# Seven more layer-1 blocks beside the gate matrix, kept in DRAM until the expert loop uses them

## The chip, the cores and the metric

The kernel runs on one core of one Trainium2 chip. The metric is the device time of one execution in microseconds. Of the kernel before there are three timed runs, and one execution was profiled; all durations below are of that one.

## The reference, cut to what matters

One encoder block over 512 tokens of width 1024: two kinds of attention, then PEER, a product-key retrieval of single-neuron experts. The change touches only PEER. Each token has 8 heads, each of which picks 16 of 128 x 128 = 16384 experts:

```python
def chunk(args):
    xc, ic, gc = args
    uc = u[ic]
    act = jnp.einsum("cd,ced->ce", xc, uc)
    hid = jax.nn.gelu(act, approximate=False) * gc
    return jnp.einsum("ce,ced->cd", hid, v[ic])
```

## The kernel before, in words

The matmuls of float32 operands are made of three products of a rounded high part (hi) and a low remainder (lo). `load_split` loads one 128x1024 tile into `raw` by SP's queue, rounds it on ScalarE (L82, `whi`) and subtracts on VectorE or GpSimd (L84, `wlo`).

PEER is computed in two ways at once. For the first 320 tokens (T1) every expert is computed densely, in 128 blocks of 128 experts. **Layer 1** of block j (`layer1`, L610) is 24 matmuls of 128x320 (L100 to L102) of `u_blk[j]` with the tokens, and a Gelu on ScalarE into a tile `ge` (L617). **Layer 2** of block j (`layer2`, L894) multiplies `ge` by the gate matrix's block (`hd`, L888), splits it into `hh` and `hl`, and adds it times `v_blk[j]` into six accumulators (18 matmuls of 128x512, L901), for 384 tokens. For the other tokens the chosen experts' rows are fetched: 64 gathers from `u_rows` (`ug` with `codeX`, VectorE's L629) for 64 tokens, whose second layer is in the dense one, and 128 gathers of u and 128 of v rows (`vg`, VectorE's L637) for the last 128 tokens.

The stages that matter here follow each other:

- **The gate stage.** The gate matrix of 384 tokens is built in 24 chunks (`ch`) of 4 groups of 4 tokens: VectorE makes one-hot tiles (`oh`, L834), GpSimd and ScalarE in turn scale them by the gate (L842, L840), TensorE multiplies them (`ps_s`, L846), ScalarE copies to `stg` (L847), and each chunk is written to DRAM (`gdram`, 1 MB). The 51 remaining `codeX` gathers are spread over the first 72 groups. Beside it layer-1 blocks are computed ahead (`backlog`); their `ge` tiles stay in SBUF, in a pool `blp` of NB = 47 buffers. 21 blocks are made before the gate stage; NG = 17 are spread over its first 80 groups, their low parts on VectorE and GpSimd in turn; NP = 5 stand between group 80 and group 81, all on GpSimd; and the last 4 behind the last group.
- Group 81 needs a transpose of `hx` (L825), the result of the `codeX` gathers. It is placed on TensorE behind the NP blocks.
- **The expert loop** (L960). For j below 47 an iteration is layer 2 alone, with `ge` from SBUF. From 47 on it also has layer 1 of the next block. Every iteration loads `v_blk` (512 KB, two buffers `raw2`, low part on VectorE) and, with 2 of 8, part of the gate tile `gtl` back from DRAM. `gather_to` (L964) paces the 256 gathers by `gw`: 1.174 in an iteration of layer 2 alone, 2.25 times that in one with layer 1. `ug` and `vg` have three buffers each.

The order on each engine is made by a scheduler at build time, which sorts by a simulated time and keeps what the waits, `issue_after` and `keep_in_program_order` demand. Each engine then runs its list strictly in order, and SP's queue does too.

## Time and profile before

| | |
|---|---|
| timed runs | 1695.65, 1700.76, 1707.4 us; median 1700.76 |
| profiled execution | 1701.23 us |
| its span, first to last instruction | 1699.2 us |
| TensorE busy in the span | 1601.0 us (94%) |
| VectorE, ScalarE, GpSimd busy | 1310.4, 807.6, 779.5 us |
| bytes moved | 407.44 MB, mean 240 GB/s |

Busy time of one engine is the union of its instructions. The matmuls of the gate stage appear as two rows each, so its 384 are 768 in the trace. A row of a window says for each engine how long it was busy in that stretch, so that busy against length shows which engine the stage runs on.

### The profile page before, as it was taken

The numbers are of one execution on the slowest core, as the hardware profiler recorded it, in microseconds if no ns is written. First come the engines' busy times: TensorE is split into PE (matmuls) and PEld (weight loads), VectorE is DVE, ScalarE is ACT, GpSimd is POOL, SyncE is SP. The second block draws the span as 40 slices with busy tenths as digits, with TensorE's granted clock in tenths as the row PEclk, the third lists the DMA queues.
The fourth block names the chain that finished last, engine by engine and source line by source line (L and its number), as shares of the span: only waits on it lengthen the run. The fifth ranks groups of instructions, "written<-read, shape, count | busy, mean of one in ns | idle before, by whom it ended". The sixth has DMA issues, their size and how long they took to land.

```text
span 1699.2 us, 25986 instructions
## 1 busy us (share of the span) xinstructions
PE 1601.0 (94%) x9390; PEld 1435.4 (84%) x9390; DVE 1310.4 (77%) x2594; ACT 807.6 (48%) x1523; POOL 779.5 (46%) x653
## 2 busy tenths in 40 slices
PE   8989999998999858889899999999999999999997
PEld 7878988788999758789778778988888888888986
DVE  7376766546799989997568887888888888888875
ACT  5446565434333248788633333444444444434334
POOL 2543221123789977776213333444444445443341
PEclk9999999999999979999999999999999999999999
DMA  7523211333222549997589999999999999999982
GB/s 249 148 57 92 83 67 50 100 99 131 86 93 92 196 167 345 346 362 272 198 284 326 327 337 319 322 345 331 353 337 344 334 355 334 343 339 316 315 295 102
DMA packets 162482, 407.44 MB, mean 240 GB/s; under 512 B 21297, under 2 KB 72881, under 8 KB 159282
## 3 DMA queue, kind: packets, MB, share of 16 engines
q1 hardware_dynamic: 114848, 235.63, 40.2%
q0 software_dynamic: 47360, 169.89, 28.7%
q8 instruction: 74, 1.21, 0.3%
q14 instruction: 54, 0.44, 0.1%
q10 hardware_dynamic: 146, 0.27, 0.0%
HBM read 374.02 MB, written 30.87 MB: 238 GB/s over the span
## 4 chain that ended last, share of the span: by engine, by line
PE 72%; DVE 12%; DMA 5%; ACT 4%; issue 4%; POOL 3%; SPq 0%; ACTq 0%; POOLq 0%; DVEq 0%
PE acc L901 29%; PE ps_mm L100 12%; PE ps_mm L102 11%; PE ps_mm L101 11%; DMA vg<-in_v_blk_dram,codeV 3%; PE ps_s L846 2%; DVE oh L834 1%; ACT stg L847 1%; DMA ug<-in_u_rows_dram,codeX 1%; PE ps_o L100 1%; PE ps_o L102 1%; PE ps_o L101 1%; ACT whi L82 1%; PE ps_t L365 1%; POOL oh L842 1%
## 5 line engine op out<-in xcount | busy, mean ns | idle before, releaser
L82 ACT ACTIVATE whi<-raw 128x1024 fp32r<-128x1024 f32 x322 | 341.4, 1061 | 475.5 <-PE ps_mm L101 197.5
L84 DVE TENSOR_TENSOR wlo<-raw,whi 128x1024 fp32r<-128x1024 f32 x234 | 287.2, 1229 | 146.1 <-ACT whi L82 144.6
L100 PE MATMUL ps_mm<-xah,whi 128*128 128x320 f32 x1152 | 361.6, 314 | 11.0 <-ACT ge L617 9.4
L102 PE MATMUL ps_mm<-xah,wlo 128*128 128x320 f32 x1152 | 359.4, 312 | 6.8 <-POOL wlo L84 4.0
L101 PE MATMUL ps_mm<-xal,whi 128*128 128x320 f32 x1152 | 358.3, 311 | 0.0
L84 POOL TENSOR_TENSOR wlo<-raw,whi 128x1024 fp32r<-128x1024 f32 x88 | 214.7, 2441 | 283.3 <-ACT whi L82 235.5
L626 POOL DMA_INDIRECT ug<-in_u_rows_dram,codeU x128 | 159.7, 1248 | 261.1 <-DVE ug L629 241.1
L634 POOL DMA_INDIRECT vg<-in_v_blk_dram,codeV x128 | 174.6, 1364 | 221.7 <-DVE yg L637 197.3
L901 PE MATMUL acc<-whi,hh 128*128 128x512 f32 x756 | 243.0, 397 | 3.0 <-ACT hh L90 3.0
L901 PE MATMUL acc<-wlo,hh 128*128 128x512 f32 x756 | 239.4, 396 | 0.0
L901 PE MATMUL acc<-whi,hl 128*128 128x512 f32 x756 | 234.4, 395 | 0.0
L100 PEld LDWEIGHTS ps_mm<-xah,whi 128*128 128x128 f32 x1152 | 218.6, 190 | 16.2 <-ACT ge L617 10.7
L102 PEld LDWEIGHTS ps_mm<-xah,wlo 128*128 128x128 f32 x1152 | 218.2, 189 | 9.5 <-POOL wlo L84 5.0
L101 PEld LDWEIGHTS ps_mm<-xal,whi 128*128 128x128 f32 x1152 | 218.6, 190 | 3.6
L637 DVE SCALAR_TENSOR_TENSOR yg<-vg,hidg,yg 128x1024 f32<-128x1024 f32 x128 | 164.2, 1283 | 9.6 <-DMA vg<-in_v_blk_dram,codeV 9.6
L901 PEld LDWEIGHTS acc<-wlo,hh 128*128 128x128 f32 x756 | 142.3, 188 | 34.8
L901 PEld LDWEIGHTS acc<-whi,hl 128*128 128x128 f32 x756 | 141.6, 188 | 34.7 <-DVE hl L92 0.4
L901 PEld LDWEIGHTS acc<-whi,hh 128*128 128x128 f32 x756 | 138.8, 188 | 31.2 <-ACT hh L90 3.5
L629 DVE SCALAR_TENSOR_TENSOR ug<-ug,xg 128x1024 f32<-128x1024 f32 x128 | 155.8, 1219 | 2.6 <-DMA ug<-in_u_rows_dram,codeU 2.6
L846 PE MATMUL ps_s<-oh 128*128 128x128 f32 x768 | 107.2, 290 | 32.8 <-POOL oh L842 16.3
L846 PEld LDWEIGHTS ps_s<-oh 128*128 128x128 f32 x768 | 98.8, 196 | 39.9 <-POOL oh L842 21.6
L90 ACT ACTIVATE hh<-hd 128x384 fp32r<-128x384 f32 x128 | 66.4, 520 | 114.1 <-DVE hd L888 113.0
(277 smaller groups left out, 2891.2 us busy)
## 6 DMA issues: line engine op xcount, KB each, us to landing
raw<-in_u_blk_dram SPq DMA_DIRECT2D x128, 512.0 KB
raw<-in_v_blk_dram SPq DMA_DIRECT2D x128, 512.0 KB
gdram<-stg SPq DMA_DIRECT2D x24, 1024.0 KB
gtl<-gdram SPq DMA_DIRECT2D x64, 384.0 KB
raw<-in_w_in_dram SPq DMA_DIRECT2D x34, 512.0 KB
raw<-in_w_q_dram SPq DMA_DIRECT2D x16, 512.0 KB
x_t<-in_x_dram SPq DMA_DIRECT2D x8, 512.0 KB
raw<-in_w_o_dram SPq DMA_DIRECT2D x8, 512.0 KB
```

Of the source, the lines that this page charges most:

```text
L82: act(hi, raw, AF.Copy)
L84: eng.tensor_tensor(out=lo, in0=raw, in1=hi.bitcast(F32), op=ALU.subtract)
L90: last_hi[0] = act(hi, src, AF.Copy, scale=scale)
L100: mm(ps, ah, bh, start=i == 0, stop=False)
L101: mm(ps, ah, bl, start=False, stop=False)
L102: last = mm(ps, al, bh, start=False, stop=i == n - 1)
L626: i_ = pool.indirect_dma_start(out=t, out_offset=None, in_=u_src, in_offset=bass.IndirectOffsetOnAxis(ap=code[:, p:p + 1], axis=0))
L629: return vec.scalar_tensor_tensor(out=t, in0=t, scalar=1.0, in1=mul, op0=ALU.mult, op1=ALU.mult, accum_out=dst[:, p:p + 1])
L634: i_ = pool.indirect_dma_start(out=t, out_offset=None, in_=v_src, in_offset=bass.IndirectOffsetOnAxis(ap=codeV[:, p:p + 1], axis=0))
L637: vec.scalar_tensor_tensor(out=yg, in0=t, scalar=hidg[:, p:p + 1], in1=yg, op0=ALU.mult, op1=ALU.add)
L846: gm = mm(ps[:, z * P:(z + 1) * P], oh[:, 0, z], oh[:, 1, z], start=True, stop=True)
L901: mm(accs[tt][hf], st_[:, ts_], mv[:, hf * S:(hf + 1) * S], start=j == 0 and st_ is hh and mv is vh, stop=False)
```

## The change

Seven more blocks, 47 to 53, are computed before the loop. SBUF keeps only the first 47; the seven go through a two-buffer tile `sge` to a DRAM tensor `sdram`, by ScalarE's own DMA queue, and `load_ge` brings each back by SP's queue two iterations ahead, into `dq`'s `ge` tile of two buffers. So the loop has 54 iterations of layer 2 alone in place of 47, and seven fewer with layer 1. Of the seven, five are spread over the first 80 groups (NG 17 to 22), one stands with the NP blocks (5 to 6), one behind the last group (4 to 5). In the spread part every third block has its low part on VectorE, where it was every second: 8 of 17 before, 8 of 22 now. `gw` rises to 256 / (54 + 2.25 x 69) = 1.223.

```diff
+NS = 7
+    sdram = dp.tile([NS, P, T1], F32, name="sdram")
-        ge = keep.tile([P, T1], F32, name="ge")
+        ge = keep.tile([P, T1], F32, name="ge") if j < NB or j >= NB + NS else stp.tile([P, T1], F32, name="sge", bufs=2)
         with tc.issue_after(last_hi[0].ins) if j < 2 else ExitStack():
             act(ge, ps[:, :T1], AF.Gelu)
+        if NB <= j < NB + NS:
+            nc.scalar.dma_start(sdram[j - NB], ge)
         return ge
...
-                if nbl[0] < NB:
+                if nbl[0] < NB + NS:
...
-        NP = 5
-        NG = NB - 4 - NP - nbl[0]
+        NP = 6
+        NG = NB + NS - 5 - NP - nbl[0]
...
-                        backlog(1, (vec, pool)[nbl[0] % 2])
+                        backlog(1, (vec, pool, pool)[nbl[0] % 3])
...
-            backlog(NB, vec)
+            backlog(NB + NS, vec)
...
-        return gelu_bl[j] if j < NB else layer1(j, dq, vec)
+        return gelu_bl[j] if j < NB else ge.pop(j) if j < NB + NS else layer1(j, dq, vec)
+
+    def load_ge(j):
+        if NB <= j < NB + NS:
+            ge[j] = dq.tile([P, T1], F32, name="ge")
+            nc.sync.dma_start(ge[j], sdram[j - NB])
...
-    gw = (2 * P) / (NB + 2.25 * (NK - NB - 5))
+    gw = (2 * P) / (NB + NS + 2.25 * (NK - NB - NS - 5))
     for j in range(NK - 1):
         cur, vcur = nxt, vnx
         vnx = vget(j + 1)
+        load_ge(j + 2)
         nxt = hidden(j + 1, get_ge(j + 1))
...
-            gather_to(int(gw * (min(j + 1, NB) + 2.25 * max(0, j + 1 - NB))))
+            gather_to(int(gw * (min(j + 1, NB + NS) + 2.25 * max(0, j + 1 - NB - NS))))
```

In the changed file the lines below `NS = 7` stand 1 to 10 lower. On GpSimd, early in the gate stage, the list before is (L842 scales a one-hot tile, L626 is a gather, L84 a layer-1 block's low part):

```order
L842 TENSOR_TENSOR oh<-oh,pk 128x512
L626 DMA ug<-in_u_rows_dram,codeX 128x1024
L84 TENSOR_TENSOR wlo<-raw,whi 128x1024
L626 DMA ug<-in_u_rows_dram,codeX 128x1024
L842 TENSOR_TENSOR oh<-oh,pk 128x512
L626 DMA ug<-in_u_rows_dram,codeX 128x1024
L842 TENSOR_TENSOR oh<-oh,pk 128x512
L626 DMA ug<-in_u_rows_dram,codeX 128x1024
L842 TENSOR_TENSOR oh<-oh,pk 128x512
L626 DMA ug<-in_u_rows_dram,codeX 128x1024 x2
L842 TENSOR_TENSOR oh<-oh,pk 128x512
```

and at the same place, with the change (L846 scales, L630 gathers, L85 is the low part):

```order
L846 TENSOR_TENSOR oh<-oh,pk 128x512
L630 DMA ug<-in_u_rows_dram,codeX 128x1024
L85 TENSOR_TENSOR wlo<-raw,whi 128x1024
L630 DMA ug<-in_u_rows_dram,codeX 128x1024 x2
L846 TENSOR_TENSOR oh<-oh,pk 128x512
L85 TENSOR_TENSOR wlo<-raw,whi 128x1024
L846 TENSOR_TENSOR oh<-oh,pk 128x512
L630 DMA ug<-in_u_rows_dram,codeX 128x1024
L846 TENSOR_TENSOR oh<-oh,pk 128x512
L630 DMA ug<-in_u_rows_dram,codeX 128x1024 x2
L846 TENSOR_TENSOR oh<-oh,pk 128x512
```

A second low part now stands among the scalings and gathers of the same stretch. On ScalarE, from the last copies of the gate stage to the first split of the loop, the list before is (`raw_9269` is the first `raw2` tile):

```order
L847 ACTIVATE stg<-ps_s 128x4x128 x2
L617 ACTIVATE ge<-ps_mm 128x320 x2
L82 ACTIVATE whi<-raw_9269 128x1024
L617 ACTIVATE ge<-ps_mm 128x320 x2
L889 ACTIVATE hd<-gtl 128x64 x2
L90 ACTIVATE hh<-hd 128x384 x2
```

and with the change, from the first write on:

```order
L621 DMA sdram<-sge 128x320
L619 ACTIVATE sge<-ps_mm 128x320
L621 DMA sdram<-sge 128x320
L619 ACTIVATE sge<-ps_mm 128x320
L621 DMA sdram<-sge 128x320
L619 ACTIVATE sge<-ps_mm 128x320
L621 DMA sdram<-sge 128x320
L619 ACTIVATE sge<-ps_mm 128x320
L621 DMA sdram<-sge 128x320
L83 ACTIVATE whi<-raw_9508 128x1024
L893 ACTIVATE hd<-gtl 128x64 x2
L91 ACTIVATE hh<-hd 128x384 x2
```

The four Gelus are five, each followed by its write, and the rounding of the loop's first v tile stands behind the last of them. On SP, in the loop's part of layer 2 alone, the list before repeats this:

```order
L80 DMA raw_10098<-in_v_blk_dram 128x1024
L80 DMA raw_10132<-in_v_blk_dram 128x1024
L873 DMA gtl<-gdram 128x6x128
L80 DMA raw_10168<-in_v_blk_dram 128x1024
L80 DMA raw_10202<-in_v_blk_dram 128x1024
L873 DMA gtl<-gdram 128x6x128
```

and with the change, where the last five spilled tiles are fetched:

```order
L81 DMA raw_11155<-in_v_blk_dram 128x1024
L929 DMA ge<-sdram 128x320
L877 DMA gtl<-gdram 128x6x128
L81 DMA raw_11192<-in_v_blk_dram 128x1024
L929 DMA ge<-sdram 128x320
L877 DMA gtl<-gdram 128x6x128
L81 DMA raw_11228<-in_v_blk_dram 128x1024
L929 DMA ge<-sdram 128x320
```

One fetch of 160 KB stands behind nearly every v load there.

## Rows read from the trace of the kernel before

**Rows 1.** Stretches: start:end, length, busy us of each engine, clock, DMA share, GB/s.

```profile
632.00:789.00 157.00, 135.10 (x977) 130.24 (x977) 150.39 (x181) 133.16 (x260) 114.87 (x99) 0.97 0.93 341
790.00:800.00 10.00, 10.00 (x78) 10.00 (x77) 4.90 (x6) 7.83 (x14) 3.42 (x2) 1.00 0.42 160
859.00:1055.00 196.00, 196.00 (x832) 156.75 (x833) 159.69 (x239) 78.68 (x142) 64.78 (x56) 0.99 0.93 319
1055.00:1500.00 445.00, 445.00 (x2427) 397.76 (x2426) 368.98 (x460) 181.13 (x294) 207.17 (x151) 1.00 0.95 338
1605.00:1680.00 75.00, 72.66 (x390) 63.48 (x388) 54.16 (x64) 30.78 (x52) 21.20 (x16) 1.00 0.69 244
```

**Rows 2.** The chain that ended last, in order of time: start, us, what.

```profile
674.42 8.25 DMA ug<-in_u_rows_dram,codeX
...
850.81 6.69 DMA gtl<-gdram
858.88 196.76 PE acc L901 x834
...
1065.46 4.19 PE acc L901 x18
1073.17 4.19 PE acc L901 x18
```

**Rows 3.** Groups from 632 to 789 us: count, busy us, mean ns, idle before and its releasers.

```profile
L846 PE MATMUL ps_s<-oh 128*128 128x128 f32 x606 | 84.6, 291 | 25.2 <-POOL oh L842 12.8 <-ACT oh L840 9.5 <-ACT stg L847 2.0
...
L629 DVE SCALAR_TENSOR_TENSOR ug<-ug,ps_x 128x1024 f32<-128x1024 f32 x50 | 60.6, 1212 | 6.6 <-DMA ug<-in_u_rows_dram,codeX 6.0 <-DVE oh L834 0.6
L626 POOL DMA_INDIRECT ug<-in_u_rows_dram,codeX x51 | 50.0, 980 | 10.0 <-issue 4.2 <-DVE oh L834 1.8 <-DVE ug L629 0.6
...
L84 POOL TENSOR_TENSOR wlo<-raw,whi 128x1024 fp32r<-128x1024 f32 x9 | 21.4, 2382 | 1.2 <-ACT whi L82 1.1
L82 ACT ACTIVATE whi<-raw 128x1024 fp32r<-128x1024 f32 x15 | 15.9, 1058 | 8.3 <-PE ps_mm L101 7.8 <-issue 0.5
```

**Rows 4.** Waits of VectorE from 632 to 789 us: total, times, longest.

```profile
DVE ug L629 <- DMA ug<-in_u_rows_dram,codeX: 6.0, 7, 1.4
```

**Rows 5.** Stretches inside the gate stage, as in rows 1.

```profile
640.00:650.00 10.00, 10.00 (x81) 10.00 (x81) 10.00 (x13) 9.33 (x20) 8.23 (x7) 1.00 0.98 358
...
750.00:760.00 10.00, 7.48 (x46) 6.94 (x45) 10.00 (x13) 7.71 (x15) 5.86 (x5) 0.83 1.01 399
```

**Rows 6.** TensorE in order of time around the NP blocks.

```profile
797.47 0.60 PE L846 MATMUL ps_s<-oh 128*128 128x128 f32 x4
...
815.95 0.27 PE L825 MATMUL ps_t<-ident,hx 128*128 128x128 f32 x1
```

**Rows 7.** ScalarE in order of time at the start of the loop.

```profile
855.93 0.44 ACT L617 ACTIVATE ge<-ps_mm 128x320 f32<-128x320 f32 x1 [2.47 <-PE ps_mm L102]
857.60 0.40 ACT L889 ACTIVATE hd<-gtl 128x64 f32<-128x64 f32 x2 [1.23 <-DMA gtl<-gdram]
...
1694.40 0.38 ACTq L954 DMA_DIRECT2D out_dram<-vg  x1
```

**Rows 8.** Stretches of the loop's part with layer 2 alone, as in rows 1.

```profile
960.00:980.00 20.00, 20.00 (x87) 15.75 (x86) 14.98 (x25) 6.75 (x13) 8.17 (x9) 1.00 0.98 347
980.00:1000.00 20.00, 20.00 (x87) 15.90 (x86) 16.54 (x25) 8.78 (x17) 7.76 (x7) 1.00 0.99 337
```

**Rows 9.** VectorE's low parts of v tiles 26 and 36, in order of time.

```profile
962.38 1.22 DVE L84 TENSOR_TENSOR wlo<-raw,whi 128x1024 fp32r<-128x1024 f32 x1 [0.68 <-ACT whi L82]
...
1008.51 1.22 DVE L84 TENSOR_TENSOR wlo<-raw,whi 128x1024 fp32r<-128x1024 f32 x1
```

**Rows 10.** DMA issues of the whole program: count, KB each.

```profile
raw<-in_v_blk_dram SPq DMA_DIRECT2D x128, 512.0 KB
...
gtl<-gdram SPq DMA_DIRECT2D x64, 384.0 KB
```

**Rows 11.** Waits of VectorE from 1560 to 1660 us.

```profile
DVE yg L637 <- DMA vg<-in_v_blk_dram,codeV: 9.6, 9, 3.3
```

## The prediction, made before the changed kernel ran

> **What bounds the kernel now.** I read the stretches first [rows 1]: who is busy for the whole of a stretch? In the expert loop it is TensorE: 196.00 of 196 us in the part with layer 2 alone, 445.00 of 445 where layer 1 is in the loop too. So an iteration there costs what its matmuls cost. The gate stage is another matter: from 632 to 789 us VectorE is busy 150.39 of 157 us, ScalarE 133.16, GpSimd 114.87, and TensorE 135.10, with DMA at a share of 0.93. VectorE sets the pace, and TensorE waits 25.2 us for the scaled one-hot tiles [rows 3]. From 790 to 800 us it turns round: TensorE 10.00 of 10, VectorE 4.90 [rows 1]. TensorE runs without a gap from the matmuls of group 80 to the transpose of `hx` [rows 6], and what is between them is the NP blocks. So the stage has two halves for this question: until group 80 TensorE has idle time, and behind it none.
>
> **What the change saves in the loop.** In the chain the 18 matmuls of a layer 2 take 4.19 us, and with layer 1 in the loop they start anew after 1073.17 - 1065.46 = 7.71 us [rows 2]. The 24 matmuls of layer 1 are the difference, 3.52 us. Seven blocks fewer, where TensorE is the bound, give 7 x 3.52 = 24.6 us. The 14 splits on ScalarE and VectorE, the seven loads of u and the Gelus go with them and were hidden under TensorE.
>
> **The same seven blocks, before the loop.**
>
> Five of them lie among groups 1 to 80. The price if TensorE hides nothing is 5 x 3.52 = 17.6 us; if it hides all, 0. TensorE has 25.2 us idle there, so 17.6 us fit, with some 8 left of 157. VectorE, the bound, gets nothing: 8 spread blocks have their low part there before and after. GpSimd gets five of 2.38 us [rows 3], 114.9 to 126.8 us; ScalarE five of 1.06 and 0.44 [rows 3, 7], 133.2 to 140.7. DMA gets 5 x 0.52 = 2.6 MB on 341 x 157 = 53.5 MB. So nothing is over 157 us, but five engines come to between 81% and 97% in strict order: a low part of 2.38 us ahead of a scaling, as the order shows, makes that group late, and the one-hot ring of five tiles only lends some time. For a small loss speaks a stretch in which all run at once: 640 to 650 us with TensorE, VectorE 10.00 of 10 and ScalarE 9.33, and DMA at 358 GB/s, which is what the stage would then need on average (56.1 MB in 157 us); 750 to 760 us even had 399 GB/s [rows 5]. VectorE waits only 6.0 us in all for gathers now [rows 4]. I take 4 us, nearer to the row of 640 us than to a full serial cost, and keep 0 and 17.6.
>
> The sixth stands among the NP blocks, where TensorE has no gap. The transpose waits for all of them, and the last 16 groups wait for the transpose: +3.5 us. There are 18 us between the two rows of TensorE [rows 6] for five blocks of 17.6. It would cost less if the spread blocks that fill TensorE from 790 us on [rows 1] came forward into its idle time by as much; I keep 0 to 3.5 and take 3.5.
>
> The seventh is behind the last group. Now the four end blocks are done with the Gelu at 855.93, and layer 2 starts at 858.88, set by the gate tile's load that lands at 857.5 [rows 2, 7]. A fifth block ends TensorE's work some 0.3 us behind the old start. But ScalarE's list has, behind that block, the Gelu (0.44), the issue of its write (0.38 by the one such issue in the trace [rows 7]), the rounding of the first v tile (1.06, which was out of the way before), and then what now takes from 857.60 to 858.88, 1.3 us. That is 3.2 us of TensorE waiting in place of the present 2.9, so the start moves by about 3.5 us less what overlaps; I take +3, and 0.3 to 3.5 as bounds. The five writes of 164 KB go out beside the gate tile's round trip and can delay it by 0.8 MB at the 341 GB/s of the gate stage, 2.4 us, to about 860: behind ScalarE's chain. Two `sge` tiles mean that a Gelu waits for the write before the last, with two blocks, 7 us, to land.
>
> **The way back through DRAM.** A `ge` tile is 164 KB. In the loop's first part a block moves 524 KB of v, 197 KB of gate tile (64 x 384 KB over 128 blocks, [rows 10]) and 1.174 gathers of 524 KB: 1.34 MB in 4.20 us, 318 GB/s, as measured (319, [rows 1]). With `gw` at 1.223 it is 324; for the seven with a fetch, 1.53 MB, 363 GB/s. From 960 to 1000 us DMA is at 0.98 and 0.99 of its time with 347 and 337 GB/s [rows 8]. That is a ceiling that holds v back: the low part of v tile 26 (counted from the loop's first) ends at 963.60 and that of tile 36 at 1009.73 [rows 9]. Layer 2 takes 834 / 18 = 46.3 blocks in 196.76 us from 858.88 [rows 2], 4.25 each with the slower start, and comes to these blocks at 969.3 and 1011.8. The lead shrank from 6 us to 2 in ten blocks. At 340 GB/s seven blocks of 1.53 MB take 31.4 us in place of 29.4, and the lead of 2 us could cover that. I take +1, and 0 to 4.
>
> The order shows each fetch behind a v load on SP, two iterations ahead (8.4 us). It waits for VectorE's `hd` of two blocks before, done by then, so it holds the next v load little. Its landing is queued work of the same DMA engines and counted above. The Trainium skill ("DMA: Bandwidth & Descriptors", Specifications) gives one core some 358 GB/s of HBM; with that the seven would take 29.9 us, the loss would be 0.5 and the sum the same to half a microsecond, but this trace shows no stretch of the loop's first part that high.
>
> **The end of the loop.** Gathers are paced 4% denser, 2.75 in place of 2.64 in an iteration of 7.71 us. From 1605 to 1680 us TensorE already loses 2.3 us [rows 1], because VectorE waits for a `vg` tile (nine waits, 9.6 us [rows 11]) with the next low part behind it in its list. I take +1, and 0 to 4.
>
> **The sum**, against the profiled execution's 1701.2 us (0.5 above the median of the three): -24.6 + 4 + 3.5 + 3 + 1 + 1 = -12.1, so **1689 us**, 0.7% less. The bounds give 1701.2 - 24.6 + 0.3 = 1676.9 at the best and 1701.2 - 24.6 + 32.6 = 1709.2 at the worst. A difference of 1%, 17 us, is about what a measurement of this kernel can tell from no change.
>
> **Rivals.**
>
> 1. *The gate stage hides all five blocks, and the DRAM way costs nothing.* For it: the 25.2 us of idle TensorE, and 640 to 650 us with all engines full. Against it: VectorE's 96%, and a v stream whose lead falls to 2 us. -24.6 + 0 + 3 + 3 + 0 + 1 = -17.6: 1684 us and down to 1677, from the edge of 1%.
>
> 2. *The five are serial after all* (the change moves work without hiding it): TensorE's list has the layer-1 matmuls in front of the groups, so a late low part from GpSimd holds the groups, VectorE fills its five one-hot tiles and stops. -24.6 + 17.6 + 3.5 + 3 + 1 + 1 = +1.5: 1703 us. With two thirds serial, 1697. Against it: the same order of lists hides 17 blocks now.
>
> 3. *Slower: the ring of `codeX` gathers.* Four `ug` tiles serve 50 gathers in 157 us, one per 3.14 us, 12.6 us for a trip round the ring. A trip needs the issue (0.98 [rows 3]), the landing (8.25 where the chain shows one [rows 2]) and VectorE's product (1.21 [rows 3]): 10.4. So 2.1 us are left. It decides from a landing of 10.4 us: each us more costs 50 / 4 = 12.5 us, since VectorE, the bound, then waits at every gather. With landings of 12 us the stage grows by 20, in place of the 4 that I take: 1705; with 13 us by 32: 1718. 5% more bytes on a DMA at 0.93 speak for some of that, the 6.0 us of waits in all, and the stretch of 399 GB/s without harm, against much. By the same 358 GB/s of the Trainium skill ("DMA: Bandwidth & Descriptors", Specifications) the stage would with the five blocks be just full, and this rival would have a better chance than I give it.
>
> **How the numbers follow.** Forecast (1684 to 1697): 0.53. Rival 1 (1677 to 1684): 0.25. Rival 2 (1697 to 1704): 0.13. Rival 3 (1704 to 1725): 0.09, of which a little over half is above 1718. Faster by over 1% (below 1684) is rival 1: 0.25; slower by over 1%: 0.05; within: 0.70. The range leaves out most of rival 3, part of rival 2 and the lowest of rival 1: 1680 to 1702.
>
> **What would show it.** In the changed profile: layer 2 starts some 6 us plus the gate stage's growth later (865 to 875 us); the transpose of `hx` 21 to 22 us behind group 80; TensorE's idle time from 632 us to group 80 down from 25 to about 12 us, with VectorE's waits for gathers below 12; 54 iterations of some 4.2 us, with at most 4 us of TensorE idle around the fetched blocks; then 7.71 us each; and 2 to 6 us idle at the end. I am wrong if VectorE waits for one-hot tiles or gathers by tens of microseconds (rivals 2, 3), or if the loop's first part is no longer full on TensorE, since then the ceiling of DMA and not the count of matmuls sets the loop.

## The result, and the profile after

The changed kernel takes 1712.3 us (median of 9, 1703.9 to 1714.4), the kernel before 1700.7 (9 runs): ratio 1.0066, 95% interval 1.0047 to 1.0085. It is 11 us slower where 12 us faster was forecast, and outside the range. The profiled execution takes 1714.3 us, with a span of 1712.5 (1699.2 before).

The stretches of the changed kernel, with the columns of [rows 1]:

```profile
636.00:809.00 173.00, 158.25 (x1163) 155.15 (x1164) 154.72 (x189) 148.24 (x282) 129.49 (x106) 0.98 0.92 335
809.00:831.00 22.00, 22.00 (x152) 21.75 (x150) 3.68 (x3) 9.30 (x14) 7.21 (x3) 1.00 0.52 178
880.00:1115.00 235.00, 228.13 (x955) 180.21 (x954) 181.89 (x271) 87.76 (x158) 78.19 (x67) 0.99 0.93 316
1125.00:1570.00 445.00, 440.34 (x2387) 391.70 (x2386) 372.07 (x467) 174.63 (x291) 218.06 (x155) 1.00 0.95 340
```

The third line is the one to see. In the loop's part with layer 2 alone TensorE was busy for 196.00 of 196 us [rows 1]; now it is 228.13 of 235. DMA has the same share, 0.93, but moves 316 GB/s in place of 319: more is asked of it and less comes.

Where the 13.3 us of the two profiled executions lie is read from seven marks on TensorE's timeline: the first score matmul of the keys, the first gate matmul, the last one ahead of the transpose of `hx` (group 80), the transpose, the first matmul of layer 2, the first of layer 1 in the loop, the last of layer 2. The stretches between them, in us:

```
                              to the  to group  to the     to        to layer 1   to the
                              gate    80        transpose  layer 2   in the loop  end
before                        205.6   166.0     17.9       42.9      196.6        633.5
after                         209.0   173.3     21.2       47.7      240.3        583.1
forecast for after            205.6   170       21.4       46        229.7        577.7
```

The first layer-1 matmul of the loop can stand ahead of the end of the last layer-2 block beside it, so the column "to layer 1" is read by its count of layer-2 matmuls. Before, it holds 834, which is 46 blocks of 18 and 6 more:

```profile
1055.24 0.39 PE L901 MATMUL acc<-whi,hl 128*128 128x512 f32 x1
1055.47 0.30 PE L100 MATMUL ps_mm<-xah,whi 128*128 128x320 f32 x1
...
1055.76 0.40 PE L901 MATMUL acc<-whi,hl 128*128 128x512 f32 x1
```

With the change it holds 972, all 54 blocks. At 4.19 us for 18 matmuls [rows 2] the 138 more take 32.1 us, so TensorE alone would make 196.6 + 32.1 = 228.7; it is 11.6 more. The last stretch should lose 7 x 7.71 = 54.0 us and the 12 matmuls that now stand ahead of its mark, 2.8 us, which makes 576.7; it is 583.1, 6.4 more.

The rest of the 13.3 us is 0.9 us ahead of the first mark, which lies anywhere from 422 to 429 us in these kernels, and 0.2 behind the last.

What holds the loop stands in the chain of waits of the changed kernel, in order of time (start, us, what):

```profile
985.32 11.21 DMA raw<-in_v_blk_dram
...
996.61 1.06 ACT whi L83
997.67 0.15 ACT hd L893
997.82 0.42 ACT hh L91
...
998.28 18.62 PE acc L905 x72
...
1026.18 8.73 DMA raw<-in_v_blk_dram
...
1034.94 1.07 ACT whi L83
...
1044.84 10.22 DMA raw<-in_v_blk_dram
```

Before, this stretch was one piece of TensorE [rows 2]. Now the chain goes through loads of v. The three shown take 8.7 to 11.2 us. There are two `raw2` tiles, so a load goes out when the low part of the load before last is done, and two blocks cost a landing and 1.06 + 1.23 us of rounding and low part. For 4.19 us a block the landing must stay below 8.4 - 2.3 = 6.1 us in the mean. From its issue on SP to the start of its rounding a load of v took 5.9 us in the mean of the kernel before's 47 and 6.0 in that of the 54: there was hardly any room in either. A single load of 8.7 us (issued at 963.63, rounded from 972.32) was borne before, with TensorE full.

TensorE has six gaps in this part, 6.7 us in all. Each ends on `hh`, as does its wait of 4.3 us ahead of the first block (total of the seven, times, longest):

```profile
PE acc L905 <- ACT hh L91: 10.9, 7, 4.3
```

Five times ScalarE had just rounded a v tile that it had waited for: in its list the rounding of a tile stands in front of `hh`. At 998.28 us block 27 starts, whose own tile was ready at 991.32; it waited behind the rounding of tile 28. The sixth time, at 1051.89, `hh` waited for a gate tile, whose load SP had sent at 1042.01, right behind a v load that had waited for its tile until 1041.63. Behind the longest gap the matmuls come 0.43 us apart in place of 0.23 for some 4 us, and the granted clock of the stretch is 0.86 of 2.4 GHz in the mean, so partly at 1.2:

```profile
1000.00:1010.00 10.00, 10.00 (x39) 7.91 (x39) 9.96 (x16) 4.56 (x9) 3.92 (x3) 0.86 0.81 272
```

Of the seven fetches two go out at 878 us and the other five from 1080.8 to 1100.4: four of the six gaps, 4.2 us, come ahead of these five.

The gate stage's groups from 636 to 809 us, and VectorE's waits there (total, times, longest):

```profile
L850 PE MATMUL ps_s<-oh 128*128 128x128 f32 x637 | 87.0, 288 | 17.9 <-POOL oh L846 10.1 <-ACT oh L844 7.3 <-ACT stg L851 0.5
...
L85 POOL TENSOR_TENSOR wlo<-raw,whi 128x1024 fp32r<-128x1024 f32 x15 | 35.9, 2395 | 3.6 <-ACT whi L83 3.4
```

```profile
DVE ug L633 <- DMA ug<-in_u_rows_dram,codeX: 8.9, 6, 3.4
DVE wlo L85 <- ACT whi L83: 3.3, 1, 3.3
```

TensorE's idle time fell from 25.2 to 17.9 us [rows 3], not to 12; VectorE's waits for gathers rose from 6.0 to 8.9 [rows 4], below the 12 that the forecast allowed. VectorE's own work did not grow. Up to group 80 it was, before,

```profile
632.00:798.00 166.00, 144.10 (x1046) 139.24 (x1047) 156.29 (x188) 139.95 (x272) 118.29 (x101) 0.97 0.91 333
```

busy for 156.29 of 166 us, and with the change for 154.72 of 173: what grew is the time in which it waits. The start of the loop on ScalarE:

```profile
874.26 0.44 ACT L619 ACTIVATE sge<-ps_mm 128x320 f32<-128x320 f32 x1 [3.08 <-PE ps_mm L103]
874.72 0.33 ACTq L621 DMA_DIRECT2D sdram<-sge  x1
875.10 1.06 ACT L83 ACTIVATE whi<-raw 128x1024 fp32r<-128x1024 f32 x1 [0.40 <-ACT sge L619]
876.06 0.39 ACT L893 ACTIVATE hd<-gtl 128x64 f32<-128x64 f32 x2
877.91 0.94 ACT L91 ACTIVATE hh<-hd 128x384 fp32r<-128x384 f32 x2 [1.46 <-DVE hd L892]
```

That is the chain of the forecast: Gelu, issue of the write, rounding of the first v tile, `hd`, `hh` [rows 7].

### The profile page after: what moved, and what is told of

Read it like the earlier page. It is cut to its first block, busy times and chain, and to the rows that moved or that the text cites. A ratio compares the mean times of both kernels' runs of the same rounds, so it can differ in the third digit from the quotient of the medians.

```text
span 1712.5 us, 26016 instructions
## 1 busy us (share of the span) xinstructions
PE 1603.8 (94%) x9390; PEld 1434.6 (84%) x9390; DVE 1298.3 (76%) x2588; ACT 806.4 (47%) x1523; POOL 798.5 (47%) x659
## 4 chain that ended last, share of the span: by engine, by line
PE 64%; DVE 15%; DMA 9%; ACT 5%; issue 5%; POOL 2%; ACTq 0%; DVEq 0%; POOLq 0%; SPq 0%
PE acc L905 17%; PE ps_mm L103 12%; PE ps_mm L101 12%; PE ps_mm L102 12%; DMA raw<-in_v_blk_dram 6%; PE ps_s L850 4%; DVE wlo L85 3%; ACT whi L83 2%; DMA vg<-in_v_blk_dram,codeV 2%; DVE eq L735 1%; DVE ug L633 1%; DVE codes L741 1%; PE ps_o L101 1%; PE ps_o L103 1%; PE ps_o L102 1%
## 5 line engine op out<-in xcount | busy, mean ns | idle before, releaser
L85 DVE TENSOR_TENSOR wlo<-raw,whi 128x1024 fp32r<-128x1024 f32 x228 | 278.1, 1227 | 177.7 <-ACT whi L83 175.3
L85 POOL TENSOR_TENSOR wlo<-raw,whi 128x1024 fp32r<-128x1024 f32 x94 | 229.2, 2440 | 287.5 <-ACT whi L83 248.3
L638 POOL DMA_INDIRECT vg<-in_v_blk_dram,codeV x128 | 181.7, 1419 | 226.0 <-DVE yg L641 190.8
L630 POOL DMA_INDIRECT ug<-in_u_rows_dram,codeU x128 | 158.5, 1238 | 255.7 <-DVE ug L633 212.0
L905 PE MATMUL acc<-whi,hl 128*128 128x512 f32 x756 | 229.4, 397 | 0.0
L641 DVE SCALAR_TENSOR_TENSOR yg<-vg,hidg,yg 128x1024 f32<-128x1024 f32 x128 | 164.0, 1282 | 11.3 <-DMA vg<-in_v_blk_dram,codeV 11.2
L850 PE MATMUL ps_s<-oh 128*128 128x128 f32 x768 | 105.4, 289 | 25.4 <-POOL oh L846 13.6
L850 PEld LDWEIGHTS ps_s<-oh 128*128 128x128 f32 x768 | 98.3, 197 | 30.9 <-POOL oh L846 16.2
L838 DVE TENSOR_TENSOR oh<-ps_t,pk 128x1024 f32<-128x1024 f32 x96 | 113.3, 1217 | 3.0 <-ACT ps_t L812 3.0
```

The lines of the kernel that those rows point to most:

```text
L85: eng.tensor_tensor(out=lo, in0=raw, in1=hi.bitcast(F32), op=ALU.subtract)
L630: i_ = pool.indirect_dma_start(out=t, out_offset=None, in_=u_src, in_offset=bass.IndirectOffsetOnAxis(ap=code[:, p:p + 1], axis=0))
L638: i_ = pool.indirect_dma_start(out=t, out_offset=None, in_=v_src, in_offset=bass.IndirectOffsetOnAxis(ap=codeV[:, p:p + 1], axis=0))
L641: vec.scalar_tensor_tensor(out=yg, in0=t, scalar=hidg[:, p:p + 1], in1=yg, op0=ALU.mult, op1=ALU.add)
L838: vec.tensor_tensor(out=oh, in0=iops.unsqueeze(1).unsqueeze(1).broadcast_to([P, 2, 4, P]), in1=pk[:, 0:2, c:c + 4].unsqueeze(3).broadcast_ ...
L850: gm = mm(ps[:, z * P:(z + 1) * P], oh[:, 0, z], oh[:, 1, z], start=True, stop=True)
```

## The experiments

Ratios are to the kernel before, with 95% intervals; 1.0066 is the change. The stretches are those of the marks, from one profiled execution of each kernel; it can lie several us off the median (after, no DRAM way: 1700.9 against 1708.6), so the ratios decide about the whole. "full" is what the layer-2 matmuls counted in the stretch "l.1" (to layer 1 in the loop) take at 4.19 / 18 us each, from the 196.6 us of the kernel before. Line by line the runs gave:

```
                                     ratio (95%)              gate   g.80   tr.   l.2   l.1    full   end
before, seven left out               0.9929 (0.9913-0.9944)   205.6  167.4  17.9  43.1  231.7  228.0  583.7
before, the same, three v tiles      0.9904 (0.9886-0.9922)   205.6  168.8  17.9  43.4  225.7  225.9  584.9
before, three v tiles from block 4   0.9992 (0.9981-1.0003)   205.5  167.9  17.9  43.6  196.2  196.6  631.1
before, 32 gathers fewer             0.9994 (0.9981-1.0007)   205.6  167.4  17.9  43.1  195.7  196.6  630.3
after, no DRAM way                   1.0054 (1.0032-1.0077)   209.7  172.5  21.2  47.3  231.8  228.0  582.5
after, old pace                      1.0042 (1.0026-1.0058)   209.9  172.4  21.2  48.2  229.3  228.0  588.0
after, three v tiles throughout      1.0088 (1.0064-1.0111)   210.1  174.7  21.3  58.6  228.5  228.0  584.1
after, three v tiles from block 4    1.0004 (0.9990-1.0019)   210.0  172.9  21.2  48.1  228.0  228.0  580.2
after, 32 gathers fewer              0.9967 (0.9947-0.9986)   209.9  175.6  21.2  47.7  227.5  225.9  576.1
after, no u (47 to 53)               1.0065 (1.0040-1.0089)   209.9  172.6  21.2  47.7  236.2  228.7  582.6
after, no u (five spread)            1.0072 (1.0046-1.0097)   209.9  171.8  21.5  46.7  236.5  228.7  585.2
after, no low parts (five spread)    1.0050 (1.0031-1.0068)   209.9  170.9  22.6  48.4  237.2  228.7  583.4
after, few matmuls (five spread)     1.0094 (1.0075-1.0113)   209.9  178.3  22.3  46.8  236.1  228.7  585.3
after, old turns                     1.0078 (1.0053-1.0103)   205.6  178.7  22.0  47.7  235.5  228.7  587.1
after, mixed turns                   1.0055 (1.0036-1.0074)   205.5  173.6  22.4  47.7  237.5  228.7  588.5
five blocks, mixed, three v tiles    0.9988 (0.9977-1.0000)   205.6  176.2  18.9  44.2  218.4  218.7  600.4
seven blocks, mixed, three v tiles   0.9988 (0.9972-1.0005)   205.6  172.9  22.4  48.2  228.0  228.3  584.3
six blocks, mixed, three v tiles     0.9975 (0.9963-0.9987)   205.6  173.1  22.4  44.6  223.3  223.6  588.4
```

The theories of the loop were "matmuls" (the forecast's), "bytes" (the loop as a whole moves 322 GB/s before and after, so only bytes count), "two v buffers" (the landings of v in a ring of two tiles) and "pace" (denser gathers).

**Seven blocks left out of the loop.**

```diff
-        return gelu_bl[j] if j < NB else layer1(j, dq, vec)
+        return gelu_bl[j] if j < NB else gelu_bl[j - 7] if j < NB + 7 else layer1(j, dq, vec)
...
-    gw = (2 * P) / (NB + 2.25 * (NK - NB - 5))
+    gw = (2 * P) / (NB + 7 + 2.25 * (NK - NB - 7 - 5))
...
-            gather_to(int(gw * (min(j + 1, NB) + 2.25 * max(0, j + 1 - NB))))
+            gather_to(int(gw * (min(j + 1, NB + 7) + 2.25 * max(0, j + 1 - NB - 7))))
```

> The kernel before, with layer 1 of blocks 47 to 53 left out of the loop altogether (the loop uses the Gelu tiles of blocks 40 to 46 a second time); the gate stage is unchanged, the gathers are paced as with the change. It shows what the change could save in the loop at the very best. Theory 'matmuls' (the forecast's): -24.6 us, near 1676, the loop from its first layer 2 to the last block about 800 us. Theory 'bytes' (the loop moves what the DMA engines can move, 322 GB/s over its whole length both before and after, so only bytes count): seven loads of u less, 3.67 MB, 3.67 / 0.322 = -11.4 us, near 1689, the loop about 813 us at 320 to 325 GB/s. Theory 'two v buffers' (only the part with layer 2 alone is held back, by the landings of v in a ring of two tiles): seven blocks at 4.5 in place of 7.71 us and 47 at 4.4 in place of 4.28, -17 us, near 1684.

-12 us, just what "bytes" said: even without any price ahead of the loop, the 24.6 us were not to be had. By the marks both parts lose: 231.7 us are 3.7 over full, and the end of 583.7 is 6.3 over the 577.4 that its matmuls would take. What holds either part this run does not tell.

**No way through DRAM.**

```diff
-            nc.scalar.dma_start(sdram[j - NB], ge)
...
-        return gelu_bl[j] if j < NB else ge.pop(j) if j < NB + NS else layer1(j, dq, vec)
+        return gelu_bl[j] if j < NB else gelu_bl[j - NS] if j < NB + NS else layer1(j, dq, vec)
...
-        load_ge(j + 2)
```

> The changed kernel without the seven writes and the seven fetches (the loop uses the Gelu tiles of blocks 40 to 46 a second time in their place); the seven blocks are still computed beside the gate matrix. Theory 'bytes': 1.15 MB of fetches less in the loop, -3.6 us there, and 1.15 MB of writes less at the end of the gate stage, 0 to -3.6 us: 1705 to 1709. Theory 'two v buffers': v comes late from block 31 on, before any fetch, so the part with layer 2 alone keeps most of its loss, -1 to -3 us: 1709 to 1711. If the way through DRAM were the whole of it: -12 us or more, 1700.

About -2 us in the whole, which the intervals don't tell from nothing. The part with layer 2 alone takes 231.8 us, 3.8 over full, as with seven left out; the seven runs that leave this part as the change has it (after, no u twice, no low parts, few matmuls, old and mixed turns) take 235.5 to 240.3, 8.3 over full in the mean. So without the fetches some 4.5 us less are lost there in this execution, the fastest of its seven, and the rest of the loss is there without them.

**Three tiles for v.**

```diff
-    vget = lambda j: load_split(v_blk[j], vec, dq)
+    vget = lambda j: load_split(v_blk[j], vec, None if j < NB + NS - 2 else dq)
```

> The changed kernel, where v of the first 52 blocks goes to the three tiles that layer 1 uses later in place of two. Theory 'two v buffers': the part with layer 2 alone is full on TensorE again, 4.25 us a block in place of 4.50, -10 to -13 us, near 1700. Theory 'bytes': a third tile adds no bandwidth; the first part may become shorter but what it draws ahead is missing behind it, the whole loop stays at 322 GB/s and 818 us: 0, between -3 and +1 us, 1709 to 1713.

No gain in the whole, as "bytes" said, but the run did two things at once: the loop was 11 us shorter and started 11 us later, since the first v loads stood behind u in the same three tiles, and the first gate tile's loads behind them in SP's list (issued from 878.4 us in place of 863.9). So it was repeated with the first four tiles as they were, in both kernels:

```diff
-    vget = lambda j: load_split(v_blk[j], vec, dq)
+    vget = lambda j: load_split(v_blk[j], vec, None if 4 <= j < NB + NS - 2 else dq)
```

> The changed kernel with three tiles in place of two for v, as in the run before, but from block 4 to block 51 only, so that the first tiles are loaded as in the changed kernel and layer 2 starts at 878 us again. Theory 'two v buffers': the part with layer 2 alone takes 228 to 231 us in place of 240.3 and what follows 583 to 585, so the whole is 8 to 12 us shorter, 1701 to 1705. Theory 'bytes': the 228.5 us of the run before came of the 11.6 us that it started later, in which gathers and v were drawn ahead; the loop takes 821 to 825 us again from its start, 0 to -3, 1709 to 1713.

> The kernel before with the same three tiles from block 4 to block 44. Its TensorE is idle for 3.8 us in the loop by the marks, all of it in the part with layer 1, where nothing is changed. Both theories: 0, between -2 and +1 us.

The whole comes down from 1.0066 to 1.0004, -10.5 us, while the kernel before gets -0.1%. "Bytes" falls for this part. With three tiles the stretch, ScalarE's waits for v in the part with layer 2 alone (total, times, longest), and the whole chain from 980 to 1060 us read:

```profile
880.00:1100.00 220.00, 220.00 (x944) 176.42 (x943) 182.34 (x268) 90.52 (x160) 84.06 (x66) 1.00 0.96 338
```

```profile
ACT whi L83 <- DMA raw<-in_v_blk_dram: 14.3, 11, 3.9
```

```profile
979.95 80.27 PE acc L905 x344
```

and the same waits in the changed kernel, with two tiles, with those for the gate tile, of which three tiles leave none:

```profile
ACT whi L83 <- DMA raw<-in_v_blk_dram: 87.4, 38, 6.0
...
ACT hd L893 <- DMA gtl<-gdram: 8.2, 2, 4.2
```

TensorE is full again, the chain is one piece of it, and the same DMA engines move 338 GB/s in place of 316, and in stretches more than the 337 to 347 that the prediction took for a ceiling:

```profile
910.00:930.00 20.00, 20.00 (x87) 16.08 (x86) 18.46 (x31) 9.09 (x16) 6.39 (x6) 1.00 1.05 381
```

What looked like their ceiling was too little work handed to them. What the third tile takes away is all that two tiles hold up: the v loads themselves and, in strict order behind them, the gate tile's loads on SP and `hh` on ScalarE. These were not separated.

**The pace of the gathers.**

```diff
-    gw = (2 * P) / (NB + NS + 2.25 * (NK - NB - NS - 5))
+    gw = (2 * P) / (NB + 2.25 * (NK - NB - 5))
+    gx = (2 * P - gw * (NB + NS)) / (NK - NB - NS - 5)
...
-            gather_to(int(gw * (min(j + 1, NB + NS) + 2.25 * max(0, j + 1 - NB - NS))))
+            gather_to(int(gw * min(j + 1, NB + NS) + gx * max(0, j + 1 - NB - NS)))
```

> The changed kernel with 1.174 gathers a block in the part with layer 2 alone, as before, in place of 1.223, and 2.79 in place of 2.75 behind it. Theory 'pace': the part with layer 2 alone gets back 8 to 12 of its 12 us, near 1702. Theory 'bytes': 2.6 gathers (1.4 MB) less in the first part, 4 us shorter, and as much longer behind it; 0, between -2 and +2 us, 1710 to 1714. Theory 'two v buffers': -2 to -4 us.

-4 us, at the edge of what "two v buffers" said, with an interval that overlaps the change's. The part with layer 2 alone takes 229.3 us, only 1.3 over full although the fetches are there, and 5 us come back in the last stretch. So three gathers fewer in 54 blocks, or no fetches, each take back much of what this part loses: the two act together, and the loss can't be shared out between them.

**32 gathers fewer, in both kernels.**

```diff
-        while sum(npu) < min(goal, 2 * P):
+        while sum(npu) < min(goal, 2 * P - 32):
...
-    gw = (2 * P) / (NB + NS + 2.25 * (NK - NB - NS - 5))
+    gw = (2 * P - 32) / (NB + NS + 2.25 * (NK - NB - NS - 5))
```

> The kernel before without the last 32 of the 256 gathers of the loop, and paced for 224; 16.8 MB less, 52 us of DMA at 322 GB/s. Theory 'bytes': the loop is then TensorE's alone, 128 x 4.19 + 81 x 3.52 = 821 us and what surrounds them, from 830 by the same marks: -3 to -9 us, 1691 to 1697. A theory in which waits of the loop come from order and buffers and not from bytes: 0 to -2.

> The changed kernel without the same 32 gathers. Theory 'bytes': the loop is TensorE's alone here too, 128 x 4.19 + 74 x 3.52 = 797 us, from 823.5 by the same marks: -22 to -27 us, 1685 to 1690, so that the change would now be a gain in the loop of the 24.6 us of the forecast, and 3 to 6 us in the whole against the kernel before with the same gathers left out. A theory in which the loss comes from order, buffers or the way through DRAM: -2 to -8 us, 1704 to 1710, and slower by 8 us or more than the kernel before with the same left out.

The kernel before gains 0.1%, the changed one 1%: with less traffic the change is a gain, of some 4 us. By the marks its loop takes 803.6 us against 826.0, -22.4 of the 24.6, and TensorE is full where it waited:

```profile
880.00:1100.00 220.00, 219.29 (x937) 175.65 (x936) 170.35 (x252) 88.13 (x156) 57.95 (x58) 1.00 0.93 316
1125.00:1570.00 445.00, 445.00 (x2427) 397.81 (x2426) 356.03 (x445) 180.20 (x292) 188.86 (x140) 1.00 0.92 327
```

So the count of matmuls in the forecast was right, and the room in DMA was not.

**Left out and three tiles.** The first run again with the third tile:

```diff
-    vget = lambda j: load_split(v_blk[j], vec, dq)
+    vget = lambda j: load_split(v_blk[j], vec, None if 4 <= j < NB + 5 else dq)
```

> The kernel before with layer 1 of blocks 47 to 53 left out of the loop, and three tiles for v from block 4 to block 51. With two tiles the loop by the marks took 815.3 us in place of 830.0, -14.7, and the ratio was 0.9929. Theory 'two v buffers': the loop saves 21 to 24 us, the whole -20 to -24, ratio 0.986 to 0.988. Theory 'bytes': 11.4 us as with two tiles, ratio 0.992 to 0.994.

-16.3 us, between the two. The part with layer 2 alone takes 225.7 us, full, so there it is the ring. In the last stretch, which still loads u and v in the old tiles, 584.9 us stay 5 above 579.5; with 32 gathers fewer nothing is lost there (630.3 - 54.0 = 576.3, measured 576.1). Whether bytes or buffers hold that stretch was not separated.

**The gate stage without loads of u.**

```diff
-    uh, ul = load_split(u_blk[j], eng)
+    uh, ul = load_split(u_blk[j], eng, raw=gbuf if NB <= j < NB + NS else None)
```

> The changed kernel without the seven loads of u for blocks 47 to 53: their splits read a tile that is in SBUF already (the final norm's weight), and splits, matmuls, Gelus, writes and fetches stay. Up to the transpose of hx the gate stage moved 318 GB/s before and after, in 184.0 and 194.6 us. Theory 'bytes': six loads less there, 3.15 MB, -9.9 us, and the stretch is 184 to 186 us again although TensorE, GpSimd and ScalarE have all the added work; the seventh gives 0 to -1.6 us; total -9 to -12, near 1701. Theory 'engines' (low parts of 2.4 us on GpSimd and layer 1 in TensorE's list make groups late, 4 us; the sixth block is serial, 3.5 us): the stretch stays at 192 to 195 us, total 0 to -3, 1708 to 1712.

172.6 us to group 80, no change, but the expectation was wrong about the place: blocks 47 and 48 are NP blocks and 49 to 53 the end blocks, none lies ahead of group 80. The run tells only that the loads of these seven cost nothing where they are. With five spread blocks (25, 28, 31, 34, 37) in their place:

```diff
-    uh, ul = load_split(u_blk[j], eng)
+    uh, ul = load_split(u_blk[j], eng, raw=gbuf if j in (25, 28, 31, 34, 37) else None)
```

> The changed kernel without the loads of u of five spread blocks (25, 28, 31, 34, 37), whose splits read a tile that is in SBUF already; everything else of them stays. The stretch to group 80 took 173.5 us in the mean of the runs with the change and 166.9 before it, at 333 GB/s both times. Theory 'bytes': 2.6 MB less, -7.9 us at 333 GB/s, the stretch is 166 to 168 us again, total -6 to -8. Theory 'engines': 172 to 175 us, total 0 to -2.

171.8 us, 1.6 under the mean of the kernels with the change (173.4): the loads are not most of it. Nor are GpSimd's low parts most of it; without those of the same five:

```diff
-    uh, ul = load_split(u_blk[j], eng)
+    uh, ul = load_split(u_blk[j], None if j in (25, 28, 31, 34, 37) else eng)
...
+        if eng is None:
+            return hi, hi
         lo = wp.tile([P, D], F32R, name="wlo")
```

> The changed kernel without the low parts of the same five blocks on GpSimd (their matmuls take the high part of u twice); loads, roundings and all 24 matmuls stay. Theory 'GpSimd' (a low part of 2.4 us ahead of a scaling makes the group late): the stretch to group 80 back to 168 to 170 us, total -3 to -6. Theory 'TensorE and the list' (the layer-1 matmuls themselves stand in front of groups): 172 to 175 us, total 0 to -1.

170.9 us, 2.5 under that mean, and 1.4 more behind group 80. And without 21 of the 24 matmuls of each:

```diff
-                                        xah[:, k], xal[:, k]) for k in range(KD)])
+                                        xah[:, k], xal[:, k]) for k in range(1 if j in (25, 28, 31, 34, 37) else KD)])
```

> The changed kernel with 3 in place of 24 matmuls for each of the five spread blocks 25, 28, 31, 34 and 37 (the first of the eight parts of the contraction alone); their loads, splits and Gelus stay. 5 x 21 / 24 x 3.52 = 15.4 us less of TensorE in the stretch to group 80. Theory 'TensorE and the list' (layer 1 stands in front of groups): the stretch at 166 to 169 us in place of 173.5, total -5 to -7. If ScalarE's roundings and Gelus or the tiles make the loss: 172 to 174, total 0 to -2.

The opposite of the expectation, 178.3 us, with TensorE waiting for GpSimd's scaled tiles, and VectorE, which makes these tiles, for gathers:

```profile
L850 PE MATMUL ps_s<-oh 128*128 128x128 f32 x629 | 93.4, 301 | 24.9 <-POOL oh L846 17.7 <-ACT oh L844 7.0
...
L633 DVE SCALAR_TENSOR_TENSOR ug<-ug,ps_x 128x1024 f32<-128x1024 f32 x51 | 61.9, 1214 | 16.2 <-DMA ug<-in_u_rows_dram,codeX 16.2
```

VectorE's 16.2 us of waiting are 7.3 more than with the change, and the stretch is 5.0 longer. So this run does not tell what the matmuls cost, and "TensorE and the list" is not decided; why the gathers came later is not shown. No run makes one cost of the five blocks the 5.9 us. What sets the stretch stays open.

**The turns.** The low parts of the spread blocks by turns of two, as before:

```diff
-                        backlog(1, (vec, pool, pool)[nbl[0] % 3])
+                        backlog(1, (vec, pool)[nbl[0] % 2])
```

> The changed kernel with the low parts of the blocks spread beside the gate matrix given to VectorE and GpSimd in turn, as before, in place of one to VectorE and two to GpSimd. Theory 'turns' (three low parts on GpSimd just ahead of the gate matrix hold up the last operations on the codes, so the first gate matmul is at 636 in place of 632 us): the first gate matmul at 631 to 633, total -3 to -5 us. Theory 'bytes': the stretch from there to the transpose of hx stays at 193 to 196 us, since the bytes are the same; VectorE has 2 or 3 more low parts of 1.2 us there, which the theory 'engines' would add. If the start of the gate matrix differs by chance from run to run: 0, between -2 and +2.

The stretch ahead of the gate matrix goes back to 205.6 us, and to the tenth: every kernel with turns of three from the start has 209.0 to 210.1 there, every other one 205.5 or 205.6. But the stretch behind it grows to 178.7 (VectorE has nine low parts there in place of six, and waits 8.1 us for roundings in place of 3.3), and the whole gains nothing. VectorE ahead of the gate matrix, in the kernel before and then with the change:

```profile
609.08 3.27 DVE L731 TENSOR_TENSOR eq<-iox,bf 128x800 bf16<-128x800 bf16 x1
612.26 0.21 DVE L785 CAST ci<-codes 128x128 int32<-128x128 f32 x1
...
614.43 1.85 DVE L731 TENSOR_TENSOR eq<-iox,bf 128x800 bf16<-128x800 bf16 x1
```

```profile
610.02 0.92 DVE L735 TENSOR_TENSOR eq<-iox,bf 128x800 bf16<-128x800 bf16 x1
610.87 2.36 DVE L789 CAST ci<-codes 128x128 int32<-128x128 f32 x1
...
614.05 5.60 DVE L735 TENSOR_TENSOR eq<-iox,bf 128x800 bf16<-128x800 bf16 x1
```

and GpSimd with the change:

```profile
610.50 2.64 POOL L85 TENSOR_TENSOR wlo<-raw,whi 128x1024 fp32r<-128x1024 f32 x1
...
615.31 2.38 POOL L85 TENSOR_TENSOR wlo<-raw,whi 128x1024 fp32r<-128x1024 f32 x1
617.65 1.69 POOL L738 TENSOR_TENSOR eqc<-eq,ccode 128x800 f32<-128x800 bf16 x1
```

The turn of the first spread block moved one low part in VectorE's list, and everything behind it fell into another phase. The cast of 0.21 us takes 2.36, until GpSimd's low part ends, but the first comparison takes 2.35 less; what remains is the second comparison, with 5.60 in place of 1.85, while GpSimd has a low part and a product of its own. Mixed turns (GpSimd, VectorE, GpSimd, then turns of three) keep both good stretches:

```diff
-                        backlog(1, (vec, pool, pool)[nbl[0] % 3])
+                        backlog(1, (vec, pool)[nbl[0] % 2] if nbl[0] < 24 else (vec, pool, pool)[nbl[0] % 3])
```

> The changed kernel with the low parts of the first three spread blocks given to GpSimd, VectorE, GpSimd, as the kernel before does, and in turns of three behind them. Theory 'turns': the first gate matmul at 630 to 633 us in place of 636, the stretch to group 80 at 172 to 175 us as with the change, total -3 to -5, 1707 to 1709. If the later start was chance, or what is saved ahead comes back in the stretch: 0, between -2 and +1.

205.5 and 173.6 us; the whole, -2 us, is within the intervals' reach of no change.

**Versions.** Mixed turns and three v tiles from block 4, with five, seven and six blocks:

```diff
-NS = 7
+NS = 5
...
-        NP = 6
-        NG = NB + NS - 5 - NP - nbl[0]
+        NP = 5
+        NG = NB + NS - 4 - NP - nbl[0]
```

> Five blocks in place of seven, all five of them spread over groups 1 to 80 (five NP blocks and four end blocks as before), with three v tiles from block 4 on and the mixed turns. From the terms measured so far: the stretch to group 80 +6.6, nothing behind it and nothing ahead of it, so layer 2 starts at 865 to 867 us. Theory 'two v buffers': the loop gives 5 x 3.52 = 17.6 less 2 to 4 us, total -7 to -9, 1692. Theory 'bytes': five loads of u less and five fetches more, 1.8 MB or 5.6 us: +1, 1700 to 1703.

> All seven blocks, with three tiles for v from block 4 on and the mixed turns. From the measured terms against the kernel before: ahead of the gate matrix 0, the stage to the transpose +10, its end +5, the loop -22: -7, 1692 to 1697. If the two repairs don't add up: 1698 to 1702.

For six, `NS = 6`, `NP = 6` and the same `NG` as with five:

> Six blocks: five spread and one NP block more, four end blocks as before, with three tiles for v from block 4 on and the mixed turns. Against the kernel before: the stage to the transpose +10, its end 0 to +1, the loop 6 x 3.52 = -21 and +3 of loss: -7 to -8, 1691 to 1696. If the loss behind the part with layer 2 alone is as in the run with five blocks (5 us): 1697 to 1700.

Six blocks are a little faster than both kernels, 0.9975 (0.9963 to 0.9987), some 4 us; the seventh, an end block, costs 3.6 us ahead of the loop (48.2 against 44.6), as much as it saves. The sum of terms was 7 to 8: the loop gives 18.4 us, as expected, but the stage pays 11.5 against the mean of the five kernels without the change, in place of 10 to 11.

## Why the prediction was wrong

**The step that failed is "The way back through DRAM".** It sized the loss of the loop's first part at +1 (0 to 4); it measured 11.6 in the profile and 8.3 in the mean of seven runs. The reading behind it was right: blocks 26 and 36 start at 969.69 and 1011.98 us, as worked out there, so the lead of v is 6 us and then 2. What failed is the step from there, "the lead of 2 us could cover that". It compared a mean of bytes with a ceiling of 340 GB/s, for the seven blocks with a fetch, and put nothing down for gathers paced 4% denser through 54 blocks. The 337 to 347 GB/s [rows 8] were no ceiling: with a third tile the loop moves 381 GB/s for 20 us, and even the kernel before moves 364 from 1020 to 1030 us, more than the 358 of which the prediction says that no stretch shows it. What holds v was the ring: two tiles, a load that waits for the low part of the load before last, 6.1 us to land against 5.9 in the mean before. And a late tile holds more than its own block: `hh` of the block ahead waits behind its rounding (at the longest gap that block's own tile had a lead of 7 us, which covered nothing), and the gate tile's loads wait behind its issue. The third tile takes all of the loss in this part away; without the fetches 3.8 us of it are left, at the old pace 1.3.

**The saving of the loop**, 7 x 3.52, was right as a count: -22.4 with 32 gathers fewer against the kernel before with the same; with the third tile -21.9, or -19.1 against the kernel before with the third tile.

**Five blocks ahead of group 80**, +4 (0 to 17.6): 5.9 in the mean (172.4 to 175.6 in seven runs against 166.0 to 168.8 in five). The size was off by 2 us, TensorE's idle time by 6. That the mechanism was a low part ahead of a scaling is not shown; without the low parts of the five blocks 2.5 of it go.

**The sixth**, +3.5: 3.3, and the transpose 21.2 us behind group 80, as said. **The seventh**, +3 (0.3 to 3.5): 4.8, since the block's 3.52 us and 1.3 of the chain add and don't overlap (TensorE waits 4.3 us for `hh` in place of 3.0).

**Not in the sum: the turns**, +3.4 in the profile, 4.3 in the other runs. The diff shows them; the prediction counted low parts by engine and not where the first one lands.

**The end of the loop**, +1 (0 to 4): 6.4, over the bound. With 32 gathers fewer nothing is lost there, with the third tile 2.8; what holds it was not separated.

The sum of the misses, 3.4 + 3.3 - 0.2 + 1.8 + 10.6 + 5.4, and 1.1 outside the marks, is the 25.4 us between -12.1 and +13.3. Rivals 2 and 3 were not what happened: the gathers of `codeX` held VectorE for 8.9 us, 2.9 more than before, and TensorE hid two thirds of the five blocks. The prediction's last sentence, the loop's first part no longer full on TensorE, came true, though not through a ceiling of DMA.

## What to carry to other kernels

Before shortening what an engine does in a loop, compute the cycle of each ring that feeds it: tiles times the block's time, less what is done between landing and the next issue, is the landing that the ring bears in the mean. Compare it with the landings in the trace, and not with a mean in GB/s: here 6.1 us stood against 5.9 while the fed engine was 100% busy. See in each list, the DMA queue's too, what stands in order behind a load that comes late. A rate at a high DMA share is a ceiling only if a deeper ring does not raise it. And count the blocks of a stretch by their matmuls, since the first matmul of the next part can stand ahead of the last block's end.

## What the runs showed of the hardware

The DMA share says little of room: 0.93 with 316 GB/s and TensorE waiting, 0.96 with 338 GB/s and TensorE full, on the same transfers. The Trainium skill ("Trainium Kernel Development and Optimization", Best Practices) advises double buffering to hide DMA behind compute; here two tiles hid landings of 5.9 us in the mean, single ones of 8.7 among them, with TensorE full, and not those of 6.0 with single ones up to 11.2.

Beside work on GpSimd VectorE's operations took longer, the cast 2.36 us in place of 0.21 and the comparison 5.60 in place of 1.85. The Trainium skill ("SBUF — State Buffer", SBUF: two separate sides) says that the two engines share a port pair as an exclusive lock for a whole instruction, on VectorE's side for operations in a two-port mode or with two inputs in SBUF; the cast ends within 0.1 us of GpSimd's low part, which agrees.

With less work for TensorE a stretch was longer: 149.06 of 174 us busy at a granted clock of 0.93 of 2.4 GHz in the mean, so partly at 1.2, against 158.25 of 173 at 0.98; ahead of its one-hot matmuls it had waited 24.9 us in place of 17.9, and VectorE had waited 16.2 us for gathers in place of 8.9. That the clock made the stretch longer is not shown.

```profile
638.00:812.00 174.00, 149.06 (x1033) 143.48 (x1033) 151.57 (x185) 144.19 (x276) 124.23 (x103) 0.93 0.90 327
```
